# A fused two-layer decoder: three-pass products ordered with the pass outermost, and one transpose moved to another PSUM bank

## Chip, core and metric

The kernel runs on one core of one Trainium2 chip, as a single program. The metric is device time in microseconds of that core; the time before is the median of three runs. Every time below is from one profiled execution unless it is called a run's time.

## The reference

The reference is a decoder of two layers over 512 tokens of 1,024 features, all in fp32. The first layer's mixer is a latent attention (low-rank queries and keys with a rotary part), the second's a sliding-window attention with 16 query heads and 4 key heads. Each mixer and each MLP is followed by a layer normalisation of a scaled residual:

```python
def _mlp(x, w_up, w_down):
    h = jax.nn.relu(x @ w_up)
    return (h * h) @ w_down

for l in range(DEPTH):                      # DEPTH = 2
    y = _mla(x, ...) if l < n_a else _swa(x, ...)
    x = _layernorm(alpha * x + y, ln_mix_g[l], ln_mix_b[l])
    x = _layernorm(alpha * x + _mlp(x, mlp_w_up[l], mlp_w_down[l]), ...)
```

The hidden width is 4,096, so the two MLPs hold most of the arithmetic. The latent attention also has `c_q = _rmsnorm(h[..., :384], g_q)`, the query latents, of which the kernel needs the transpose.

## The kernel before, in words

**Three passes.** TensorE multiplies in a reduced fp32 format, so each fp32 operand is split into a high and a low part (`split`, line 74: ScalarE copies the high part on line 76, VectorE subtracts it from the source on line 79 and so makes the low part). A product is then three matmuls, which `three` (line 107) lists and `group` (line 101) issues in that order: stationary high with moving high, stationary high with moving low, stationary low with moving high. Nearly every matmul of the kernel is issued by line 103 in `group`. The names in the trace are the tiles' names: `wh` and `wl` are the high and low part of a weight tile, `xth` and `xtl` those of the transposed activations, `fac` holds both parts of a factor of the hidden activations.

**The MLP.** One level of a seven-product block scheme is used for each of four blocks of the hidden width (`Block`, line 682), for the up products of all four and the down products of the first three; the fourth block's down product is a plain one (`TokMajor`). A step of kind U with number n (`up`, line 701) makes one of the seven up products of a block: 128x128 pieces of the weight are stationary and 256 columns of activations move; it takes two weight tiles, each of eight pieces, so it issues 48 matmuls into two PSUM banks, one for each weight tile. A step of kind D (`down_`, line 760) makes one of the seven down products: pieces of the factor are stationary and 512 columns of a weight tile move; it takes two weight tiles and two row tiles t of 128 tokens, and issues 24 matmuls into two banks, one for each row tile. Before, `up` ran over four output pieces j (two to a weight tile), in each over four contraction pieces k, and for each k the three passes. `down_` ran over the row tile t, in it over four contraction pieces m (the first two from the first weight tile, the other two from the second), and for each m the three passes; behind the twelve matmuls of one t it read that bank out with VectorE (lines 548 and 551 for the residual, 778 and 781 for a partial sum kept in `u2`).

**The order of the steps** is written out by hand in `STEPS`, `FIRST_STEPS` and `LAST_STEPS` (lines 39 and 40). Each MLP begins with U1 U2 U5 U3 U6 U7 D2 U4 D1 of block 0, then U1 of block 1, D5 of block 0, U2, D3, U5 and so on. In the text a step is named by its kind and number, and by the layer (A the first, B the second).

**Weight tiles** come through a ring of four pairs `wh` and `wl` (`tiles_of_weights`, line 116). A raw tile is loaded by a DMA from the SP queue, or grown in place by an accumulating DMA from the POOL queue (line 184); then it is split. `weights` (line 293) prepares tiles up to four ahead on the ring. All matmuls stand in the order of the program; the other engines' instructions are put in order when the program is built, by a planner that uses its own estimates of time.

**PSUM.** There are six product banks (tag mm, `bank`, line 65) and two for transposes (tag tr, `tbank`, line 68). U6 uses the two transpose banks, all other steps product banks. VectorE combines the banks of U5, U3 and U6 on lines 736 to 742 (line 737 reads U5's banks, line 739 U3's).

**Where layer B begins.** `begin` (line 567) makes the shared keys and the first queries with `feat_major` (line 561): three chunks of weights, for each of two halves of the tokens, eight contraction pieces of 256 columns in two groups of four. Transposes of the last token tiles, which make the end of `x2`'s `xth` and `xtl`, are put between these groups.

**The third latents.** `normed_t` (line 875) transposes the query latents, three features pieces f of 128; f = 0 and 1 in one call, f = 2 in the next. Each piece takes a transpose bank, is scaled by ScalarE (line 880) and has its low part made by VectorE (line 881).

Of the kernel before, what the change touches and what calls it, by code (L numbers as in the profile page):

```python
# [2 lines left out]

# [12 lines left out]
P = 128  # L16
D = 1024
S = 512
NT = S // P
KD = D // P  # L20
# [28 lines left out]
def build(tc, nc, io, out):  # L49
    with ExitStack() as top:  # L50
# [17 lines left out]
        def tbank():  # L68
            return bank(512, "tr", 2)
# [31 lines left out]
        def group(dst, pairs, first=True, last=True, **kw):  # L101
            for i, (st, mv) in enumerate(pairs):
                pe(nc.tensor.matmul(  # L103
                    dst, st, mv, start=first and i == 0, stop=last and i == len(pairs) - 1, **kw
                ))

        def three(sh, sl, mh, ml):
            return [(sh, mh), (sh, ml), (sl, mh)]


        stream, off_ring = [], []
# [218 lines left out]
        b = bank()  # L330
# [227 lines left out]
            add_plain(t, c, b)  # L558
            count(t, c)

        def feat_major(src, w, dst, cols=slice(0, S), ks=range(KD)):
            wh, wl = w
            for k in ks:
                kc = slice(k * P, (k + 1) * P)
                group(dst, three(wh[:, kc], wl[:, kc], src.h(k, cols), src.l(k, cols)), k == 0, k == KD - 1)

        def begin(src, chunks):


            ws = [weights(name) for name, _ in chunks]  # L570
            for half_ in range(2):
                cols = slice(half_ * 256, half_ * 256 + 256)
                for i, (_, evac) in enumerate(chunks):
                    b = bank(256)
                    early = half_ == 0 and i == len(chunks) - 1
                    feat_major(src, ws[i], b, cols, range(4))
                    if early:
                        with tc.high_priority():
                            last = src.turn(NT - 1, bank)
                    feat_major(src, ws[i], b, cols, range(4, KD))  # L580
                    evac(cols, b)
                    if half_ == 0 and i == 1:
                        with tc.high_priority():
                            src.turn(NT - 2)
                if half_ == 0:
                    with behind(last):
                        prepare(1)
            state["hold"] = len(stream)


        class Factors:
# [9 lines left out]
            def sum(self, n, a11, a12, a21, a22):  # L601
                if n == 5:
                    self.a = self.scratch()
                    nc.vector.tensor_sub(self.a, a21, a22)
                    return self.a
                if n == 3:
                    nc.vector.tensor_sub(self.a, self.a, a11)
                    self.b = self.scratch()
                    nc.vector.tensor_add(self.b, a12, self.a)
                    return self.b  # L610
                if n == 7:
                    nc.vector.tensor_sub(self.b, a11, a21)
                    return self.b
                return {1: a11, 2: a12, 4: a22, 6: self.a if n == 6 else None}[n]
# [49 lines left out]
        def mlp(src, gb, dst, mp):  # L664
# [17 lines left out]
            class Block:  # L682
# [18 lines left out]
                def up(self, n):  # L701
                    w = [weights("up") for _ in range(2)]
                    key = {3: 3}.get(n) or own_bank[n]
                    for j in range(4):

                        b = self.bank(("U", key), j // 2)
                        wh, wl = w[j // 2]
                        for k in range(4):
                            c = slice(j % 2 * 512 + k * P, j % 2 * 512 + (k + 1) * P)
                            group(  # L710
                                b[:, j % 2 * 256 : j % 2 * 256 + 256],
                                three(wh[:, c], wl[:, c], src.part(n, 0)[:, k, :], src.part(n, 1)[:, k, :]),
                                n not in (2, 4) and k == 0 and j % 2 == 0, k == 3, skip_group_check=True,
                            )
                        if j % 2:
                            self.up_out(n, j // 2)
                        if (self.q, j) == (0, 1) and n in (1, 2):
                            with tc.high_priority():
                                src.turn(n + 1)

# [39 lines left out]
                def down_(self, n):  # L760
                    w = [weights("down") for _ in range(2)]
                    f = self.fac.pop(n)
                    key = {3: 5}.get(n) or own_bank[n]
                    if self.q == 0 and n == 2:
                        key = 2
                    for t in range(2):
                        tk = slice(t * P, (t + 1) * P)
                        b = self.bank(("D", key), t)
                        for m in range(4):
                            wh, wl = w[m // 2]  # L770
                            c = slice(m % 2 * 512, (m % 2 + 1) * 512)
                            group(
                                b, three(f[:, 0, m, tk], f[:, 1, m, tk], wh[:, c], wl[:, c]),
                                (n not in (2, 3, 4) or key == 2) and m == 0, m == 3, skip_group_check=True,
                            )
                        add = add_scaled if self.q == 0 else add_plain
                        if n == 1 and self.q == 0:
                            nc.vector.tensor_copy(u2[t], b)
                            add_plain(t, lows, b)
                        elif n in (1, 6):  # L780
                            nc.vector.tensor_add(u2[t], b, u2[t])
                        elif n == 2:
                            add(t, lows, b)
                        elif n == 5:
                            add(2 + t, highs, b)
                        elif n == 3:
                            add(t, highs, b)
                        elif n == 7:
                            take(2 + t, highs, b)
                        elif n == 4:  # L790
                            add(2 + t, lows, b)
# [53 lines left out]
        with tc.tile_pool(name="mla", bufs=1) as mp:  # L845
# [28 lines left out]

            def normed_t(nrm, fs, g, dst_h, dst_l):
                for f in fs:
                    pt = tbank()
                    for t in range(NT):
                        pe(nc.tensor.transpose(pt[:, t * P : (t + 1) * P], nrm[t][:, f * P : (f + 1) * P], ident))
                    nc.scalar.activation(dst_h[:, f, :], pt, AF.Copy, scale=g[:, f : f + 1])  # L880
                    nc.vector.scalar_tensor_tensor(
                        dst_l[:, f, :], pt, g[:, f : f + 1], f32(dst_h[:, f, :]), ALU.mult, ALU.subtract
                    )
# [160 lines left out]
            for t in range(NT):  # L1044
                tk = slice(t * P, (t + 1) * P)
                b = bank()
# [403 lines left out]
```

## Time and profile before

| what | before |
|---|---|
| median of three runs | 1002.6 us (1002.33 to 1003.85) |
| the profiled execution's own time | 1002.69 us |
| its span, first to last instruction | 1000.9 us |
| TensorE matmul busy | 988.5 us, 99% of the span |
| VectorE, ScalarE, GpSimd busy | 77%, 55%, 24% |
| mean granted TensorE clock | 0.997 of full speed |

Two instructions of one engine overlap in the profile where the second begins before the first has ended, as matmuls do; the distance between the starts of neighbouring matmuls is therefore what tells the pace, and a longer distance than usual is a stall. In a timeline row the first number is the start in microseconds from the span's start, the second the time covered, x the number of instructions merged, and a bracket holds the idle time of the engine just before and what ended it.

### The profile page before, as it was taken

How to read it: one execution, taken by the hardware profiler on the slowest of the kernel's cores; microseconds unless marked ns; L12 is line 12 of the kernel's file. 1: busy time of each engine (PE TensorE's matmuls, PEld its weight loads, DVE VectorE, ACT ScalarE, POOL GpSimd, SP SyncE). 2: the span in 40 equal slices, each digit the busy share in tenths (PEclk: the TensorE clock that was granted, in tenths of full speed). 3: DMA queues.
4: the chain of work that ended last, by engine and by line, in shares of the span. 5: the costliest groups of instructions: out<-in, count | busy, mean ns of one | idle time of the engine just before them, and what ended most of it. 6: DMA issues, size and time to landing. Idle time of an engine off the chain costs nothing. (4 is left out here: it accounts for less than half of the span.)

```text
span 1000.9 us, 15857 instructions
## 1 busy us (share of the span) xinstructions
PE 988.5 (99%) x6148; PEld 891.6 (89%) x6148; DVE 767.3 (77%) x1231; ACT 555.0 (55%) x847; POOL 236.0 (24%) x208
## 2 busy tenths in 40 slices
PE   9999999999999999999999999999999999999996
PEld 9888888998999999998899988889988999999986
DVE  6588866989769769886584678788995986898746
ACT  5556643467537637646146688546673664664610
POOL 1231101312212211210024565233122122123002
PEclk9999999999999999999999999999999999999998
DMA  7421125388978977973323211439698798798332
GB/s 260 143 87 43 64 106 190 84 191 236 186 168 229 185 175 203 221 125 112 120 67 113 85 64 54 153 79 228 172 217 196 167 215 175 162 262 147 83 126 84
DMA packets 60246, 149.55 MB, mean 149 GB/s; under 512 B 5211, under 2 KB 9740, under 8 KB 60172
## 3 DMA queue, kind: packets, MB, share of 16 engines
q0 software_dynamic: 24320, 58.73, 32.7%
q1 hardware_dynamic: 35852, 89.82, 26.1%
q8 instruction: 48, 0.79, 0.3%
q14 instruction: 26, 0.21, 0.1%
HBM read 146.41 MB, written 4.22 MB: 150 GB/s over the span
## 5 line engine op out<-in xcount | busy, mean ns | idle before, releaser
L103 PE MATMUL mm<-wh,fac 128*128 128x512 f32 (+1 forms) x944 | 293.1, 387 | 0.0
L76 ACT ACTIVATE wh<-wq 128x1024 fp32r<-128x1024 f32 x164 | 173.7, 1061 | 189.6 <-PE mm L103 126.3
L79 DVE TENSOR_TENSOR wl<-wq,wh 128x1024 fp32r<-128x1024 f32 x164 | 199.5, 1221 | 76.7 <-ACT wh L76 75.8
L103 PE MATMUL mm<-xth,wh 128*128 128x256 f32 (+1 forms) x936 | 244.9, 289 | 0.0
L103 PE MATMUL mm<-xth,wl 128*128 128x256 f32 (+1 forms) x808 | 234.6, 290 | 0.0
L103 PEld LDWEIGHTS mm<-wh,fac 128*128 128x128 f32 x944 | 176.2, 188 | 35.7 <-DVE fac L79 0.6
L103 PE MATMUL mm<-xtl,wh 128*128 128x256 f32 (+1 forms) x680 | 198.8, 292 | 0.3 <-DVE xtl L79 0.3
L103 PE MATMUL mm<-wl,fac 128*128 128x512 f32 (+1 forms) x472 | 182.6, 387 | 1.0 <-DVE wl L79 1.0
L103 PEld LDWEIGHTS mm<-xth,wh 128*128 128x128 f32 x936 | 170.3, 192 | 3.0
L103 PEld LDWEIGHTS mm<-xth,wl 128*128 128x128 f32 x808 | 154.8, 192 | 2.3
L184 POOL DMA_DIRECT2D wq<-in_up x64 | 77.5, 1219 | 244.6 <-DVE wl L79 179.2
L103 PEld LDWEIGHTS mm<-xtl,wh 128*128 128x128 f32 x680 | 130.2, 192 | 3.5 <-DVE xtl L79 0.7
L76 ACT ACTIVATE wh<-raw 128x1024 fp32r<-128x1024 f32 (+2 forms) x81 | 81.8, 1015 | 78.6 <-PE mm L103 57.6
L103 PEld LDWEIGHTS mm<-wl,fac 128*128 128x128 f32 x472 | 88.8, 188 | 18.3 <-DVE wl L79 1.7
L79 DVE TENSOR_TENSOR wl<-raw,wh 128x1024 fp32r<-128x1024 f32 (+2 forms) x60 | 72.4, 1218 | 33.3 <-ACT wh L76 32.7
L184 POOL DMA_DIRECT2D wq<-in_down x48 | 42.0, 875 | 204.9 <-DVE wl L79 182.2
L391 POOL TENSOR_TENSOR rs<-v,half 128x1 f32<-128x1 f32 x24 | 28.7, 1197 | 191.1 <-DVE v L410 156.1
L79 POOL TENSOR_TENSOR wl<-raw,wh 128x1024 fp32r<-128x1024 f32 (+2 forms) x21 | 43.8, 2092 | 72.6 <-ACT wh L76 72.6
L103 PE MATMUL mm<-wh,oh 128*128 128x512 f32 x128 | 51.0, 398 | 0.7 <-ACT p L1252 0.7
L103 PE MATMUL mm<-wh,ol 128*128 128x512 f32 x128 | 50.1, 391 | 0.0
L103 PE MATMUL mm<-wl,oh 128*128 128x512 f32 x128 | 49.9, 390 | 0.0
L551 DVE TENSOR_TENSOR x<-mm,x 128x512 f32<-128x512 f32 (+1 forms) x53 | 35.7, 676 | 13.8 <-PE mm L103 13.5
(227 smaller groups left out, 1834.8 us busy)
## 6 DMA issues: line engine op xcount, KB each, us to landing
wq<-in_up POOLq DMA_DIRECT2D x64, 512.0 KB, 8.5
wq<-in_down POOLq DMA_DIRECT2D x48, 512.0 KB, 7.3
wq<-in_up SPq DMA_DIRECT2D x32, 512.0 KB, 5.6
raw<-in_down SPq DMA_DIRECT2D x28, 512.0 KB, 6.5
wq<-in_down SPq DMA_DIRECT2D x24, 512.0 KB, 7.4
raw<-in_up SPq DMA_DIRECT2D x16, 512.0 KB, 5.8
raw<-in_w_o SPq DMA_DIRECT2D x8, 512.0 KB, 3.3
raw<-in_w_so SPq DMA_DIRECT2D x8, 512.0 KB, 3.5
```

The lines of the kernel that those rows point to most:

```text
L76: high = nc.scalar.activation(dst_h, src, AF.Copy)
L79: low = (engine or nc.vector).tensor_sub(dst_l, src, f32(dst_h))
L103: pe(nc.tensor.matmul(dst, st, mv, start=first and i == 0, stop=last and i == len(pairs) - 1, **kw))
L184: nc.gpsimd.dma_start(half(a, jp), chunk(*more, jp), accum_op=ALU.add)
L391: nc.gpsimd.tensor_tensor(r, v, half, ALU.pow)
L551: nc.vector.tensor_add(xs[t][:, c], b, xs[t][:, c])
```

## The change

In `up`, `down_` and the products of `begin` the pass becomes an outer loop. In `up` the order is now weight tile, pass, output piece j, contraction piece k. In `down_` it is weight tile i, pass p, row tile t, contraction piece m within the weight tile; so both row tiles' banks are open through the whole step, and both are read out behind its last matmul. In `begin` each group of four contraction pieces is issued pass by pass. The number, shapes and operands of all matmuls stay. In `normed_t` the piece f = 2 takes a product bank and no longer a transpose bank.

```diff
+        def by_pass(chunks):
+
+            return [chunk[n] for n in range(3) for chunk in chunks]
...
-        def feat_major(src, w, dst, cols=slice(0, S), ks=range(KD)):
+        def feat_major(src, w, dst, cols=slice(0, S), ks=range(KD), order=lambda chunks: sum(chunks, [])):
             wh, wl = w
+            chunks = []
             for k in ks:
                 kc = slice(k * P, (k + 1) * P)
-                group(dst, three(wh[:, kc], wl[:, kc], src.h(k, cols), src.l(k, cols)), k == 0, k == KD - 1)
+                chunks.append(three(wh[:, kc], wl[:, kc], src.h(k, cols), src.l(k, cols)))
+            group(dst, order(chunks), ks[0] == 0, ks[-1] == KD - 1)
...
-                    feat_major(src, ws[i], b, cols, range(4))
+                    feat_major(src, ws[i], b, cols, range(4), by_pass)
...
-                    feat_major(src, ws[i], b, cols, range(4, KD))
+                    feat_major(src, ws[i], b, cols, range(4, KD), by_pass)
...
                     key = {3: 3}.get(n) or own_bank[n]
-                    for j in range(4):
-
-                        b = self.bank(("U", key), j // 2)
-                        wh, wl = w[j // 2]
-                        for k in range(4):
-                            c = slice(j % 2 * 512 + k * P, j % 2 * 512 + (k + 1) * P)
-                            group(
-                                b[:, j % 2 * 256 : j % 2 * 256 + 256],
-                                three(wh[:, c], wl[:, c], src.part(n, 0)[:, k, :], src.part(n, 1)[:, k, :]),
-                                n not in (2, 4) and k == 0 and j % 2 == 0, k == 3, skip_group_check=True,
-                            )
-                        if j % 2:
-                            self.up_out(n, j // 2)
-                        if (self.q, j) == (0, 1) and n in (1, 2):
+                    for i in range(2):
+                        b = self.bank(("U", key), i)
+                        wh, wl = w[i]
+                        for p in range(3):
+                            for j, k in product(range(2), range(4)):
+                                c = slice(j * 512 + k * P, j * 512 + (k + 1) * P)
+                                group(
+                                    b[:, j * 256 : j * 256 + 256],
+                                    three(wh[:, c], wl[:, c], src.part(n, 0)[:, k, :], src.part(n, 1)[:, k, :])[p : p + 1],
+                                    n not in (2, 4) and (p, j, k) == (0, 0, 0), (p, k) == (2, 3), skip_group_check=True,
+                                )
+                        self.up_out(n, i)
+                        if (self.q, i) == (0, 0) and n in (1, 2):
                             with tc.high_priority():
                                 src.turn(n + 1)
...
+                    for i, p, t, m in product(range(2), range(3), range(2), range(2)):
+                        tk, c, k = slice(t * P, (t + 1) * P), slice(m * 512, (m + 1) * 512), 2 * i + m
+                        wh, wl = w[i]
+                        group(
+                            self.bank(("D", key), t), three(f[:, 0, k, tk], f[:, 1, k, tk], wh[:, c], wl[:, c])[p : p + 1],
+                            (n not in (2, 3, 4) or key == 2) and (i, p, m) == (0, 0, 0), (i, p, m) == (1, 2, 1),
+                            skip_group_check=True,
+                        )
                     for t in range(2):
-                        tk = slice(t * P, (t + 1) * P)
                         b = self.bank(("D", key), t)
-                        for m in range(4):
-                            wh, wl = w[m // 2]
-                            c = slice(m % 2 * 512, (m % 2 + 1) * 512)
-                            group(
-                                b, three(f[:, 0, m, tk], f[:, 1, m, tk], wh[:, c], wl[:, c]),
-                                (n not in (2, 3, 4) or key == 2) and m == 0, m == 3, skip_group_check=True,
-                            )
...
-                    pt = tbank()
+                    pt = bank() if f == 2 else tbank()
```

## Rows read from the trace of the kernel before

**Rows 1.** The page's part 1: busy time, share of the span and instructions of each engine.
```profile
PE 988.5 (99%) x6148; PEld 891.6 (89%) x6148; DVE 767.3 (77%) x1231; ACT 555.0 (55%) x847; POOL 236.0 (24%) x208
```
**Rows 2.** Waits of TensorE: us in total, times, longest us.
```profile
PE mm L103 <- DVE wl L79: 1.0, 2, 0.8
```
**Rows 3.** Timeline of TensorE, from layer A's first D5 into the U2 behind it.
```profile
248.26 0.50 PE L103 MATMUL mm<-wl,fac 128*128 128x512 f32 x1 [0.76 <-DVE wl L79]
...
252.26 0.28 PE L103 MATMUL mm<-xth,wh 128*128 128x256 f32 x1
252.38 0.28 PE L103 MATMUL mm<-xtl,wh 128*128 128x256 f32 x1
252.50 0.28 PE L103 MATMUL mm<-xth,wl 128*128 128x256 f32 x1
```
**Rows 4.** Stretches of a step each: length, then busy time (instructions) by engine.
```profile
245.56:252.26 6.70, 5.94 (x26) 4.43 (x25) 5.68 (x7) 6.33 (x7) 1.32 (x2) 1.00 1.11 255
729.67:735.68 6.01, 5.77 (x27) 4.44 (x25) 5.67 (x7) 5.96 (x7) 1.73 (x2) 1.00 1.10 258
258.02:263.49 5.47, 5.47 (x27) 4.51 (x26) 3.49 (x5) 3.68 (x4) 2.92 (x3) 1.00 1.02 187
252.26:258.02 5.76, 5.76 (x50) 5.75 (x48) 5.76 (x6) 3.56 (x4) 1.24 (x2) 1.00 1.00 183
199.89:205.84 5.95, 5.95 (x51) 5.82 (x49) 5.12 (x8) 5.74 (x8) 1.20 (x1) 1.00 1.06 302
683.94:689.95 6.01, 6.01 (x50) 5.82 (x49) 5.25 (x8) 5.86 (x8) 1.20 (x1) 1.00 1.06 306
```
**Rows 5.** Timeline of VectorE, the split before each late matmul of D5, layers A and B.
```profile
246.98 1.23 DVE L79 TENSOR_TENSOR wl<-wq,wh 128x1024 fp32r<-128x1024 f32 x1 [1.02 <-ACT wh L76]
...
730.41 1.22 DVE L79 TENSOR_TENSOR wl<-wq,wh 128x1024 fp32r<-128x1024 f32 x1 [0.34 <-ACT wh L76]
```
**Rows 6.** Timeline of VectorE and TensorE at U5 of layer B and in `begin`.
```profile
683.46 1.29 DVE L79 TENSOR_TENSOR xtl<-uv,xth 128x512 fp32r<-128x512 f32 x2
...
521.52 0.28 PE L103 MATMUL mm<-xth,wh 128*128 128x256 f32 x1
522.15 0.39 PE L103 MATMUL mm<-xtl,wh 128*128 128x256 f32 x1 [0.34 <-DVE xtl L79]
522.37 0.28 PE L103 MATMUL mm<-xth,wl 128*128 128x256 f32 x1
```
**Rows 7.** Timeline of TensorE at the third latents' transposes.
```profile
45.69 0.40 PE L103 MATMUL mm<-wh,ckv_l 128*128 128x512 f32 x1
46.26 0.66 PE L879 MATMUL tr<-ident,p 128*128 128x128 f32 x4 [0.17 <-DVE cq_l L881]
```
**Rows 8.** Timeline of VectorE and TensorE where D2 of layer B begins.
```profile
707.04 0.68 DVE L737 TENSOR_TENSOR uv<-mm,uv 128x512 f32<-128x512 f32 x1
707.23 0.40 PE L103 MATMUL mm<-wh,fac 128*128 128x512 f32 x1
```
**Rows 9.** Timeline of VectorE and TensorE around the last D4 of layer B.
```profile
947.75 0.69 DVE L551 TENSOR_TENSOR x<-mm,x 128x512 f32<-128x512 f32 x1
949.26 0.69 DVE L551 TENSOR_TENSOR x<-mm,x 128x512 f32<-128x512 f32 x1 [0.82 <-PE mm L103]
949.87 1.22 DVE L79 TENSOR_TENSOR wl<-raw,wh 128x1024 fp32r<-128x1024 f32 x1
951.00 1.22 DVE L79 TENSOR_TENSOR fac<-a,fac 128x1024 fp32r<-128x1024 f32 x1
...
952.27 0.73 PE L103 MATMUL mm<-wh,fac 128*128 128x512 f32 x2
```
**Rows 10.** Waits of all engines, then a split and its step in the middle of layer A.
```profile
ACT wh L76 <- PE mm L103: 186.1, 133, 5.8
...
341.95 1.23 DVE L79 TENSOR_TENSOR wl<-wq,wh 128x1024 fp32r<-128x1024 f32 x1 [1.76 <-ACT wh L76]
...
347.77 0.40 PE L103 MATMUL mm<-wh,fac 128*128 128x512 f32 x1
```

More of the change, by code (lines that the diff above doesn't have):

```diff
@@ L1 @@
 import math
+from itertools import product
 from contextlib import ExitStack
```

## The prediction

> **What bounds the kernel now.** The first view is the share of busy time by engine: TensorE's matmuls cover 99% of the span, no other engine more than 77% [rows 1]. That view can't show how fast the matmuls follow each other, so the second is TensorE's timeline, read by starts. In U2 of layer A neighbouring matmuls of 256 columns start 0.12 us apart [rows 3], and the step of 48 takes 5.76 us, 0.120 each; D3, 24 matmuls of 512 columns, takes 5.47 us, 0.228 each [rows 4]. Almost all steps run at these two paces, so TensorE is the bound and the change, which adds and removes no matmul, can win only what stands between matmuls. The third view, TensorE's waits, shows how little that is: it waits 1.0 us in all for low parts of weights, two times [rows 2], and the other waits are below a microsecond. So the question is which of these stalls the new order hides and whether it opens others.
>
> **The change, part by part.** The sum is made against the profiled execution, 1002.69 us (span 1000.9); the median of the runs is 1002.6, so 0.1 comes off at the end.
>
> *1. Down products, D5 of block 0.* It takes 6.70 us in layer A and 6.01 in layer B, against 5.47 for a free step: 1.23 and 0.54 us are lost [rows 4]. The late matmul starts at 248.26 behind 0.76 us of idleness, released by VectorE's low part [rows 3]; that split ran from 246.98 for 1.23 us, to 248.21 [rows 5]. It is the step's eighth matmul: row tile 0 has used the first weight tile in its first six and now wants the second tile's low part. In the new order the first tile feeds twelve matmuls, and the second tile's low part is wanted at the seventeenth: 245.56 + 16 x 0.228 = 249.21, which is 1.0 us behind its readiness. In layer B it is ready at 730.41 + 1.22 = 731.63 [rows 5] and wanted at 729.67 + 3.65 = 733.32. Both stalls go: 1.77 us. Bounds: nothing, if the splits slip by more than those leads, up to 1.77; I take 1.77, because the leads of 1.0 and 1.7 us are larger than anything that I find added in front of the splits below. What is late next? Behind D5 the splits run far ahead again: a split in the middle of layer A ends at 341.95 + 1.23 = 343.18 for a step that starts at 347.77, a lead of 4.6 us, and ScalarE's high parts wait 186.1 us in all for TensorE to give ring tiles back [rows 10]. TensorE holds the splits up there, not they it.
>
> *2. Up products, U5 of block 0.* It takes 5.95 and 6.01 us against 5.76: 0.19 and 0.25 lost [rows 4]. Here the low part of the activations is late: in layer B VectorE makes two from 683.46 for 1.29 us [rows 6], to 684.75, the first about 684.15, and the step starts at 683.94 with the low part wanted by its second matmul. In the new order eight matmuls come first, 8 x 0.12 = 0.96 us, so it is wanted at 684.90, behind even the second. Gain 0.44; bounds 0 and 0.44. In all other U steps the weights' low part is wanted 14 matmuls later than before and the high part is given back seven matmuls earlier (its last use, the 23rd matmul of a tile's 24, becomes the 16th); nothing waits there now, so this is costed at nothing.
>
> *3. The first products of layer B.* From 521.52 to the second matmul at 522.15 are 0.63 us where 0.12 is the pace, and the next distance is 0.22: 0.61 lost, released by a low part of activations [rows 6]. Pass by pass that low part is wanted by the fifth matmul, 521.52 + 0.48 = 522.00, still 0.15 early. So 0.15 stays, and perhaps the 0.10 behind it: gain 0.36 to 0.46, I take 0.40.
>
> *4. The third latents.* The four transposes start 0.57 us behind the matmul before them, where 0.23 is the pace; the release is VectorE's low part of the latents before, which frees the transpose bank [rows 7]. A product bank needs no such wait if one of the six is free. Gain 0 to 0.34; I take 0.34, since among TensorE's stalls around this place none was released by the reading of a product bank.
>
> Parts 1 to 4: 1.77 + 0.44 + 0.40 + 0.34 = 2.95 us.
>
> *5. Two banks at once in a down step.* Row tile 1's bank is wanted by the third matmul, not the thirteenth: 10 x 0.228 = 2.3 us earlier. In the regular order a bank has been read out a whole step before. The tight place is D2 of block 0, which follows U6 and U7, whose banks VectorE is still reading: in layer B the second read of U5's banks runs from 707.04 for 0.68 us, to 707.72, and D2 starts at 707.23, so its third matmul comes at 707.69 [rows 8]. Which bank the planner gives can't be seen before; and TensorE will be there up to 0.25 earlier (part 2). So 0 to about 0.5 us a layer; I take 0.15 for each, 0.30, because the read ends almost exactly when it is wanted.
>
> *6. Read-outs behind the step.* Row tile 0's read-out, 0.69 us of VectorE, moves from the middle of the step to its end, next to row tile 1's. In the middle of an MLP this lies beside splits that lead by 4.6 us [rows 10], so it costs nothing; without that cover it would cost up to 0.69 a step. At the last D4 there is no cover. The read-outs run at 947.75 and 949.26, then a weight's and a factor's low part, the latter until 951.00 + 1.22 = 952.22, and TensorE takes it up at 952.27 [rows 9]. The first read-out can now start two matmuls ahead of the second, about 949.26 - 0.46 = 948.80. Two in a row at a distance of 0.60 then end the pair about 0.15 later, and the factor with it. Two layers: 0.30; bounds 0 and 2 x 0.69 = 1.38.
>
> By this sum the change gives 2.95 - 0.30 - 0.30 = 2.35 us: 1002.69 - 2.35 = 1000.34, and 1000.3 beside the median. Every queue keeps its instructions: no DMA is added, and SP's and POOL's loads hang on splits that come no later than now, apart from what part 6 says.
>
> **A rule against it.** The rows show that the read-out of one row tile now runs beside the other row tile's matmuls, and that the splits lead by more than that read-out takes. The Trainium skill, "Perfetto Trace Analysis", section "Matmuls", asks that independent groups rotate through PSUM banks, so that the read-out of one overlaps the matmuls of the next; the change gives half of that up. By that rule each of the 42 down steps (seven in three blocks of two layers) would lay one read-out of 0.69 us open, 29 us in all, and the sum would be 1002.69 + 29 - 2.95, about 1029. The rows speak against the full price: the group behind a D step uses other banks, and the overlap is with that. What is left of the rule is the second rival.
>
> **The rivals.**
>
> *Given back, no difference.* The stalls move. For: the leads at the start of each MLP are 1 us, VectorE's read-outs are bunched, and with all of parts 5 and 6 at their upper ends (1.0 + 1.38) the gain is 2.95 - 2.38 = 0.57, so 1002.1. The same follows where D5's stall stays in part: the two read-outs behind D2 and D1 (D1's row tile 0 has two, so 0.69 + 1.37 = 2.06) pushing D5's second split past its lead of 1.0 in layer A would leave most of the 1.23. Against: that split waits for ScalarE [rows 5], so VectorE has a free place in front of it. This rival includes that the change does less than it says, since only D5's stalls are waits for a low part of weights. Between 1000.6 and 1004.6, most likely near 1001.7. Chance 0.35.
>
> *Slower, by read-outs in front of splits.* Place: VectorE's queue in the first nine steps of each MLP. If its fixed order puts both read-outs of D2, D1 and D5 ahead of splits that are wanted at once, each step pays in full: 0.69 + 1.37 + 0.69 = 2.75 a layer, 5.5 in all, against 2.95 gained: 1002.69 + 2.55 = 1005.2. It decides where a split's lead is below the read-out's 0.69 us. For: D5's lead is nearly nothing today. Against: the new order itself adds over 2 us to that lead (parts 1 and 2), and elsewhere it is 4.6. Chance 0.12.
>
> **How the numbers follow.** The forecast case, 999.4 to 1000.6, has the remaining 0.53; its lower end is 1002.6 - 3.2, all stalls of parts 1 to 4 gone with the 0.25 left in part 3. About 0.2% (2.0 us) is what a measurement of this kernel can tell from no change, so faster means below 1000.6: 0.53, within 0.35, slower 0.12. The range runs from 999.2 to 1003.0: it takes in the forecast and nearly all of the first rival and leaves out the second. The forecast's own range is 999.4 to 1000.6.
>
> **What would show it.** In the profile after: D5 of block 0 at 5.47 us in both layers, with no wait of TensorE for a weight's low part (part 1); U5 of block 0 at 5.76 (part 2); one wait of some 0.15 us at the first products of layer B (part 3); no wait at the third latents (part 4). A wait of TensorE for VectorE's line 737 or 739 at the third matmul of D2 would price part 5, and a later factor split behind the last D4 part 6. The forecast is wrong if the paces of 0.120 and 0.228 us change with the order of the passes, or if new waits of TensorE for splits, factors or banks add up to more than 0.9 us, where the gain falls below 2.0.

## The result, and the profile after

The changed kernel takes 1011.2 us (median of four runs, 1009.82 to 1012.48) against 1002.6: a ratio of 1.0083, 95% interval 1.0067 to 1.0099. It is slower, and well outside the range of the prediction. The profiled execution is the longest of the four, 1012.48 us, its span 1010.7, at the same mean clock (0.997).

TensorE still covers nearly all of the span and the number of its instructions is the same. Page, part 1, of the kernel after, against [rows 1]:

```profile
PE 990.4 (98%) x6148; PEld 891.1 (88%) x6148; DVE 766.6 (76%) x1231; ACT 552.2 (55%) x847; POOL 236.0 (23%) x208
```

The paces have not changed: a free U step still takes 48 x 0.120 us, a D step 24 x 0.228. So the loss lies between the matmuls. Take each distance between the starts of two neighbouring matmuls, less the usual (median) distance for the size of the first (0.120 us for 256 columns, 0.227 for 512), and add the differences up: 12.0 us before, 21.8 after. That is 9.8 us more, and the profiled executions differ by 1012.48 - 1002.69 = 9.8. Of it 4.9 and 5.0 us are in the U and D steps of layers A and B; the rest cancels. What is lost at a place, here and below, is counted in this way. TensorE's waits, of the kernel after, name the new stalls (us in total, times, longest us), against [rows 2]:

```profile
PE mm L104 <- DVE u L787: 5.1, 4, 1.3
PE mm L104 <- DVE uv L743: 2.4, 2, 1.4
...
PE mm L104 <- ACT fac L77: 1.0, 3, 0.5
...
PE mm L104 <- ACT wh L77: 0.5, 1, 0.5
```

No wait for a weight's low part is left, as predicted. But there are three others in the MLPs. (Line numbers moved: VectorE's split is now line 80, ScalarE's 77, the reads of the banks of U6, U5 and U3 are lines 742, 743 and 745, the partial sum's read-out 787.)

**First, D2 waits for D1.** In blocks 1 and 2 D2 adds onto the banks that D1 has just filled, after VectorE has added the partial sum to `u2` (line 787). Timelines of TensorE and then VectorE, kernel after, from the end of U4 of block 1 into D2 (a row's x4 are the four matmuls of one pass over one weight tile):

```profile
307.75 1.12 PE L104 MATMUL mm<-xth,wl 128*128 128x256 f32 x8
309.12 1.20 PE L104 MATMUL mm<-wh,fac 128*128 128x512 f32 x4 [0.25 <-ACT fac L77]
...
313.78 1.07 PE L104 MATMUL mm<-wh,fac 128*128 128x512 f32 x4
316.15 1.25 PE L104 MATMUL mm<-wh,fac 128*128 128x512 f32 x4 [1.30 <-DVE u L787]
```
```profile
307.20 1.22 DVE L80 TENSOR_TENSOR wl<-raw,wh 128x1024 fp32r<-128x1024 f32 x1 [0.48 <-ACT wh L77]
308.90 0.69 DVE L751 TENSOR_TENSOR a<-mm,uv 128x512 f32<-128x512 f32 x1 [0.48 <-PE mm L104]
309.51 2.35 DVE L80 TENSOR_TENSOR fac<-a,fac 128x1024 fp32r<-128x1024 f32 x2
...
314.18 1.22 DVE L80 TENSOR_TENSOR wl<-wq,wh 128x1024 fp32r<-128x1024 f32 x1
315.32 1.28 DVE L787 TENSOR_TENSOR u<-mm,u 128x512 f32<-128x512 f32 x2
```

D1's last matmul starts at about 314.46 and D2's first would follow 0.23 us later. It comes at 316.15, because it must follow the read-out, and a weight's split (314.18) stands in front of the read-out (315.32) in VectorE's queue: 1.46 us lost here, 1.40, 1.45 and 1.42 at the other three places, 5.7 in all. Before, the read-out of row tile 0 lay beside D1's matmuls of row tile 1, and that of row tile 1 beside D2's matmuls of row tile 0. VectorE's timeline, kernel before, same place:

```profile
312.82 0.69 DVE L781 TENSOR_TENSOR u<-mm,u 128x512 f32<-128x512 f32 x1
...
314.66 0.68 DVE L781 TENSOR_TENSOR u<-mm,u 128x512 f32<-128x512 f32 x1
```

**Second, U7 of the last block waits for U5's banks.** Timelines of ScalarE, VectorE and TensorE, kernel after, at U6 and U7 of layer A's last block:

```profile
451.01 1.06 ACT L77 ACTIVATE wh<-wq 128x1024 fp32r<-128x1024 f32 x1 [1.63 <-DMA wq<-in_up]
```
```profile
450.55 0.68 DVE L742 TENSOR_TENSOR uv<-tr,uv 128x512 f32<-128x512 f32 x1
452.10 1.23 DVE L80 TENSOR_TENSOR wl<-wq,wh 128x1024 fp32r<-128x1024 f32 x1 [0.87 <-ACT wh L77]
453.24 0.68 DVE L743 TENSOR_TENSOR uv<-mm,uv 128x512 f32<-128x512 f32 x1
```
```profile
454.07 1.19 PE L104 MATMUL mm<-xth,wh 128*128 128x256 f32 x8 [0.95 <-DVE uv L743]
```

Between the reads of U6's and U5's banks stands a split that waits for ScalarE, which waits for a load. Before, the two reads stood side by side. VectorE's timeline, kernel before, same place:

```profile
446.01 0.69 DVE L736 TENSOR_TENSOR uv<-tr,uv 128x512 f32<-128x512 f32 x1 [0.68 <-PE tr L103]
446.74 0.69 DVE L737 TENSOR_TENSOR uv<-mm,uv 128x512 f32<-128x512 f32 x1
```

Lost: 1.10 us in layer A, 1.59 in B.

**Third, D1 waits for its factor** (at 309.12 above, and at the other three D1 of blocks 1 and 2), 0.4 to 0.5 us each with the matmul behind, 1.8 in all. ScalarE's timeline, kernel after: the raw weight tile of D2 (306.13), wanted only at 316, and a square (307.08, line 754) that D5 will use go ahead of the high part of D1's factor (the first half of the row at 308.02; the second is D2's factor), wanted at 308.7.

```profile
306.13 1.04 ACT L77 ACTIVATE wh<-raw 128x1024 fp32r<-128x1024 f32 x1
307.08 1.04 ACT L754 ACTIVATE a<-a 128x1024 f32<-128x1024 f32 x1
308.02 1.99 ACT L77 ACTIVATE fac<-a 128x1024 fp32r<-128x1024 f32 x2
```

D5 of block 0 answers to [rows 4]: in layer A its stall became a wait for its factor (0.66 us, and 0.11 behind it); in B it is gone. (The first stretch begins one matmul, 0.12 us, before the step would.)

```profile
245.96:252.34 6.38, 5.88 (x28) 4.62 (x27) 6.35 (x7) 6.32 (x8) 0.86 (x1) 1.00 1.10 267
...
200.42:206.18 5.76, 5.76 (x50) 5.76 (x49) 4.94 (x8) 5.55 (x8) 1.13 (x1) 1.00 1.06 304
688.85:694.61 5.76, 5.76 (x51) 5.76 (x50) 4.99 (x8) 5.61 (x8) 1.20 (x1) 1.00 1.06 302
```

The second and third row are U5 of block 0 in both layers, now free steps of 5.76 us.

### The profile page after: what moved, and what is told of

It reads as the page before. It is cut to its first block, busy times and chain, and to the rows that moved or that the text cites. A ratio compares the mean times of both kernels' runs of the same rounds, so it can differ in the third digit from the quotient of the medians.

```text
span 1010.7 us, 15861 instructions
## 1 busy us (share of the span) xinstructions
PE 990.4 (98%) x6148; PEld 891.1 (88%) x6148; DVE 766.6 (76%) x1231; ACT 552.2 (55%) x847; POOL 236.0 (23%) x208
## 4 chain that ended last, share of the span: by engine, by line
PE 49%; issue 32%; POOL 8%; DMA 4%; DVE 4%; ACT 2%; POOLq 0%; SPq 0%; DVEq 0%; ACTq 0%
PE mm L104 45%; POOL wq L189 7%; DMA wq<-in_up 2%; DVE wl L80 1%; DMA wq<-in_down 1%; ACT wh L77 1%; PE tr L1102 1%; PE tr L1278 1%; PE tr L648 1%; PE tr L104 1%; DMA xw<-in_xT 1%; PE tr L1280 0%; ACT p L1258 0%; DMA raw<-in_w_qr 0%; DMA raw<-in_w_h 0%
## 5 line engine op out<-in xcount | busy, mean ns | idle before, releaser
L104 PE MATMUL mm<-wh,fac 128*128 128x512 f32 (+1 forms) x944 | 254.2, 388 | 6.3 <-DVE u L787 5.1
L104 PEld LDWEIGHTS mm<-wh,fac 128*128 128x128 f32 x944 | 173.3, 188 | 43.1 <-ACT fac L77 8.9
L104 PE MATMUL mm<-xth,wh 128*128 128x256 f32 (+1 forms) x936 | 143.9, 290 | 2.4 <-DVE uv L743 2.4
L104 PE MATMUL mm<-wl,fac 128*128 128x512 f32 (+1 forms) x472 | 141.3, 386 | 0.0
L104 PEld LDWEIGHTS mm<-xth,wh 128*128 128x128 f32 x936 | 124.9, 191 | 6.7 <-issue 2.7
L104 PE MATMUL mm<-xth,wl 128*128 128x256 f32 (+1 forms) x808 | 128.4, 290 | 0.0
L104 PE MATMUL mm<-xtl,wh 128*128 128x256 f32 (+1 forms) x680 | 110.6, 292 | 0.0
L104 PEld LDWEIGHTS mm<-xth,wl 128*128 128x128 f32 x808 | 107.9, 192 | 2.3
L104 PEld LDWEIGHTS mm<-xtl,wh 128*128 128x128 f32 x680 | 91.4, 192 | 1.9 <-DVE xtl L80 0.2
```

The source lines that it names most:

```text
L104: pe(nc.tensor.matmul(dst, st, mv, start=first and i == 0, stop=last and i == len(pairs) - 1, **kw))
```

## The experiments

The theory after the result had two parts. *Bank*: D2 of blocks 1 and 2 can't start until D1's banks are read, and the new order of the down products puts both read-outs behind D1's last matmul. *Queue*: the new order of the up products gives the high part of a weight tile back seven matmuls earlier; ring tiles come free sooner, and the planner then puts splits that are not yet wanted ahead of reads and factors that are. Rivals were that passes outermost are slow in themselves, or that VectorE and ScalarE simply have no room.

In the first four, what is put back is as in the kernel before. Line numbers differ by a few between the kernels.

### The up products alone

```diff
-                    for i, p, t, m in product(range(2), range(3), range(2), range(2)):
+                    for t in range(2):
...
-                    feat_major(src, ws[i], b, cols, range(4), by_pass)
+                    feat_major(src, ws[i], b, cols, range(4))
...
-                    pt = bank() if f == 2 else tbank()
+                    pt = tbank()
```

> Only the up products go pass by pass; down products, the first products of layer B and the third latents as before. Theory (queue): giving high parts of weights back earlier moves splits ahead of read-outs in the fixed queues of VectorE and ScalarE, and this belongs to the up order alone: the waits at U7 of the last block (1.1 and 1.6 us) and at D1 of blocks 1 and 2 (some 1.8 us in all) stand here too, the waits of D2 for D1's read-outs do not, and D5 of block 0 still stalls; 1002.6 + 2.7 + 1.8 - 0.4 = 1006.7 us. Rival (read-outs): all of the loss comes from reading both banks out behind a down step: then nothing is lost here and U5's 0.4 us is won, 1002.2 us.

Measured: 1010.2 us, ratio 1.0071 (1.0058 to 1.0085). Timeline of TensorE in this kernel, D1 of block 1:

```profile
308.53 0.50 PE L104 MATMUL mm<-wh,fac 128*128 128x512 f32 x1
...
310.33 0.73 PE L104 MATMUL mm<-wh,fac 128*128 128x512 f32 x2 [1.06 <-DVE fac L80]
```

The four D1 of blocks 1 and 2 lose 6.4 us to waits for their factor (7.2 with the 0.11 behind each), more than in the changed kernel, because the old order of the down products wants the factor's low part at the third matmul and not the ninth. U7 loses only 0.20 and 0.25. So the queue's price was larger than expected (1006.7), and it sat mostly at D1 and not at U7. D5 of block 0, expected to stall as before, loses only 0.18 us in layer A (1.14 in the kernel before) and 0.56 in B.

### The down products alone

The loop of `up`, the calls in `begin` and the bank of the third latents are put back; `down_` stays new:

```diff
-                        for p in range(3):
-                            for j, k in product(range(2), range(4)):
...
+                    for j in range(4):
...
+                        for k in range(4):
```

> Only the down products go weight tile by weight tile; all else as before. Theory (bank): D2 of blocks 1 and 2 adds onto D1's banks and must wait until VectorE has read D1's partial sum, four waits of 1.4 us, 5.7 in all, and D5's 1.8 us are won: 1002.6 + 5.7 - 1.8 = 1006.5 us, with no wait at U7 or for D1's factor. Rival (read-outs): the whole loss is here, near 1011 us, with the waits at U7 and D1 as well.

Measured: 1009.8 us, 1.0070 (1.0055 to 1.0086). TensorE's waits in this kernel:

```profile
PE mm L104 <- DVE u L788: 1.7, 4, 0.4
PE mm L104 <- ACT fac L77: 1.5, 2, 0.8
```

D2's four waits are there (0.58 us lost at each, 0.15 more at the matmuls behind). But they make less than 3 us: here the split in front of the read-out starts 1.2 us before D1's last matmul (314.11 and 315.31) and is over in time, in the changed kernel 0.3 before it. The other part is at D5 of block 0, where the wait for a weight's low part has become one for the factor: 0.86 and 0.97 us at its first matmul, 0.36 and 0.35 at its ninth. Stalls in the two MLPs rise by 4.5 us, outside them by 1.3; the profiled execution is the shortest of the four runs (1008.53 us), so 1.2 us of the median's loss are not in this trace. The total lies between the two expectations: the bank is confirmed as a place, not as the whole loss.

The two losses do not add up: 7.6 and 7.1 us apart, 8.6 together. Together D1 loses 1.8 us and not 6.4, while D2's waits grow from 2.9 to 5.7 and those of U7 from 0.45 to 2.7.

### The first products of layer B and the third latents alone

The loops of `up` and `down_` are put back, the rest of the change stays:

```diff
-                    for i in range(2):
...
-                        for p in range(3):
+                    for j in range(4):
...
-                    for i, p, t, m in product(range(2), range(3), range(2), range(2)):
...
                     for t in range(2):
...
+                        for m in range(4):
```

> Only the first products of layer B go pass by pass and the third latents take a product bank; up and down products as before. Both theories: the gains of 0.4 and 0.3 us stand by themselves, 1001.9 us, with a wait of about 0.15 us left in the first products. If either is taken back, 1002.6 us.

Measured: 1002.1 us, 0.9993 (0.9984 to 1.0002). In the trace the wait at the third latents is gone, and at the first products 0.25 of 0.61 us is left, as expected. By the ratio this gains 0.7 us, less than a measurement can tell from none.

### The same, and the new order only in U5 and D5 of block 0

```diff
+                    if (n, self.q) == (5, 0):
+                        self.up_passes(n)
+                    else:
+                        self.up_pieces(n)
...
+                    if (n, self.q) != (5, 0):
+                        self.down_rows(n)
+                    else:
+                        self.down_tiles(n)
```

> As e3_begin_f2, and the new order in U5 and D5 of block 0 alone, the two steps of each layer that stalled before. Theories queue and bank: neither price is paid, because no D2 follows a D1 in the new order and nearly all high parts are given back where they were, so the whole of the forecast gain comes, 1002.6 - 2.9 = 999.7 us. If D5's stall is not a matter of order but of when its second tile arrives, it stays at some 1 us in layer A and the time is 1000.7 to 1001.5 us.

Measured: 1000.6 us, 0.9975 (0.9966 to 0.9985): faster than both kernels, but 0.9 us above what was expected and next to the range named for a D5 that stays late (1000.7 to 1001.5). The trace decides: no stall of over 0.15 us is left in D5 and U5 of block 0. Timelines of VectorE and TensorE in this kernel, D5 of layer A:

```profile
247.46 1.23 DVE L80 TENSOR_TENSOR wl<-wq,wh 128x1024 fp32r<-128x1024 f32 x1 [0.94 <-ACT wh L77]
```
```profile
246.12 1.09 PE L104 MATMUL mm<-wh,fac 128*128 128x512 f32 x4
...
249.78 1.07 PE L104 MATMUL mm<-wl,fac 128*128 128x512 f32 x4
```

The split of the second tile ends at 248.69 and is wanted at 249.78: a lead of 1.1 us.

### The order of two instructions in the queues

The up products alone (the first experiment), with two instructions placed behind the split of D1's factor at the U4 of blocks 1 and 2. `behind` only orders the instructions of a queue.

```diff
-                    w = [weights("up") for _ in range(2)]
+                    late = self.pair if n == 4 and 0 < self.q < NFF - 1 else None
+                    w = [weights("up")]
+                    with behind(late):
+                        w.append(weights("up"))
...
-                        self.up_out(n, i)
+                        with behind(late if i else None):
+                            self.up_out(n, i)
...
-                    split(f[:, 0], f[:, 1], g[2] if n == 0 else self.down.sum(n, *g))
+                    self.pair = split(f[:, 0], f[:, 1], g[2] if n == 0 else self.down.sum(n, *g))
```

> The new order in the up products everywhere (as in the run with it alone, 1010.2 us), and at the four U4 of blocks 1 and 2 two instructions go behind the split of D1's factor in their queues: the split of the raw weight tile that D2 will use, and VectorE's second read-out of U4. Nothing else is moved; no matmul, load or buffer changes. Theory (the early give-back only spoils the order of the queues): TensorE's waits for the factor at D1, 6.5 us in that run, go, and the time falls to about 1003.7 (1003.0 to 1005.0). Rival (the factor is late because ScalarE and VectorE are loaded more at that place, or the pass order itself costs time): the waits stay or move behind D1, to D2's weights, and the time stays at 1009 to 1010.5.

Measured: 1006.3 us, 1.0030 (1.0018 to 1.0042), against 1.0071 without the edit; the intervals do not meet. The losses at D1 fall from 6.4 to 1.45 us. What is left is order in the queues again, with another instruction. Timelines of ScalarE and TensorE in this kernel:

```profile
306.47 1.99 ACT L758 ACTIVATE a<-a 128x1024 f32<-128x1024 f32 x2
308.36 1.04 ACT L77 ACTIVATE fac<-a 128x1024 fp32r<-128x1024 f32 x1
309.31 1.04 ACT L77 ACTIVATE wh<-raw 128x1024 fp32r<-128x1024 f32 x1
```
```profile
310.72 0.73 PE L104 MATMUL mm<-wh,fac 128*128 128x512 f32 x2 [0.53 <-DVE fac L80]
```

The raw tile (309.31) is now behind the high part of D1's factor (308.36). But two squares stand ahead of it (306.47), of which D1 needs one; the kernel before makes the other, which D5 will use, behind that factor (at 309.45, the factor at 306.60). So the factor's low part comes 0.7 us too late for D1's third matmul (310.72), and less than that at the other three D1. The time is 1.3 us above the upper end of what was expected; 0.55 and 0.28 us are lost at U7, 0.35 at D2 of block 0 in layer B, and the first 20 us took 1.1 us longer than in the first experiment's profile.

### Passes outermost, but the high part used to the end

The up products alone again, with the passes taken in another order:

```diff
-                        for p in range(3):
+                        for p in (0, 2, 1):
...
-                                    n not in (2, 4) and (p, j, k) == (0, 0, 0), (p, k) == (2, 3), skip_group_check=True,
+                                    n not in (2, 4) and (p, j, k) == (0, 0, 0), (p, k) == (1, 3), skip_group_check=True,
```

> The new order in the up products everywhere, but the three passes of a weight tile taken as high by high, low by high, high by low, so that the weight's high part is used to the tile's end, as before, and its low part is wanted at the ninth matmul. Theory (giving the high part back seven matmuls earlier is what lets splits move ahead): the queues' order stays that of before, D1 has its factor as before, and the time is that of before less the 0.44 us of U5: about 1002.3 (1001.8 to 1003.0). Rival (passes outermost are slower in themselves, or the release has nothing to do with it): 1008 to 1010.

Measured: 1002.8 us, 1.0003 (0.9994 to 1.0012). The whole loss of 7 us is gone with the early release, although the passes are still outermost. VectorE's timeline of this kernel at D1 of block 1: the factor's low part (307.45) is again ahead of the second read-out of U4 and of the raw tiles.

```profile
307.45 2.36 DVE L80 TENSOR_TENSOR fac<-a,fac 128x1024 fp32r<-128x1024 f32 x2 [0.50 <-ACT fac L77]
309.73 0.69 DVE L751 TENSOR_TENSOR a<-mm,uv 128x512 f32<-128x512 f32 x1
310.33 2.35 DVE L80 TENSOR_TENSOR wl<-raw,wh 128x1024 fp32r<-128x1024 f32 x2
```

This edit also moves the use of the low part from a tile's seventeenth matmul to its ninth. No wait for a weight's low part loses over 0.5 us in either kernel, so that does not explain 7 us.

### D2 in banks of its own

The changed kernel, with:

```diff
-                    if self.q == 0 and n == 2:
+                    if n == 2:
                         key = 2
...
                             nc.vector.tensor_add(u2[t], b, u2[t])
+                            if n == 1:
+                                add_plain(t, lows, b)
```

> The changed kernel, but D2 adds onto no bank of D1 any more: in all blocks it has banks of its own, as in block 0, and VectorE adds D1's banks into the output a second time (eight read-outs more in all, 0.69 us each). Theory (D2 waits until VectorE has read the partial sum out of D1's bank, 1.4 us at each of four places): these 5.7 us go, and 1011.2 falls to about 1005.5 (1005 to 1007). Rival (VectorE is simply behind at that place, so that any bank or factor wanted there comes late): the waits move to the next step's banks or to D5's factor, and the time stays above 1009.

Measured: 1005.8 us, 1.0027 (1.0016 to 1.0039), against 1.0083: the 5.7 us are gone at D2 of blocks 1 and 2, as expected, though VectorE does eight read-outs more. TensorE's waits in this kernel show where one came back:

```profile
PE mm L104 <- DVE uv L743: 3.4, 3, 1.3
```

Two are the U7 from above (1.09 and 1.49 us lost); the third is D2 of block 0 in layer B, 1.29 us lost at its first matmul for U5's bank.

### All three repairs

The last experiment's kernel with the edit of the queues from above, and the low part of one weight tile of the last block's U4 (the split in front of line 743) made by GpSimd (`low` is handed on to `split`; those lines are left out here):

```diff
-            4: lambda jp: grown("a", jp),
+            4: lambda jp: grown("a", jp, low=nc.gpsimd if jp in late else None),
...
-            add = {("U", q): queue_seven("up", "U", up(q)) for q in range(NFF)}
+            add = {("U", q): queue_seven("up", "U", up(q), (0,) if q == NFF - 1 else ()) for q in range(NFF)}
```

> The changed kernel with three repairs: D2 in banks of its own; at U4 of blocks 1 and 2 the raw tile's split and the second read-out behind the split of D1's factor; and the low part of one weight tile of the last block's U4 made by GpSimd and not by VectorE, so that U5's banks are read without a split between. Theory: 1011.2 less 5.7 (D2), 1.8 (D1) and 2.7 (U7) is 1001.0 (1000.3 to 1002.0), level with the run that has the new order in D5 and U5 of block 0 alone. Rival (VectorE has no room for the new order, whichever instruction stands where): the waits come back at other places and the time stays above 1004.

Measured: 1002.0 us, 0.9993 (0.9984 to 1.0002), just above the upper end of what was expected and 9.2 us below the changed kernel. TensorE's longest waits in it:

```profile
PE mm L104 <- POOL zeros L334: 1.4, 1, 1.4
PE mm L104 <- ACT p L1264: 0.7, 1, 0.7
PE mm L104 <- DVE ql L80: 0.6, 2, 0.3
```

All three are outside the MLPs, and in the kernel before too. So VectorE and ScalarE have room for the new order; the order of their queues and one pair of banks cost the time. But this is no better than the kernel before, and 1.4 us behind the one whose MLPs use the new order at two steps of a layer.

## Why the prediction was wrong

**The step that failed first** is in part 5: "In the regular order a bank has been read out a whole step before." It holds for every pair of down steps that share banks but D1 and D2 of blocks 1 and 2, which stand next to each other. The code says so: n = 2 takes D1's key except in block 0, and 787 reads the bank in between. The prediction priced two banks at once only at D2 of block 0 (0.30 us); no wait came there in the changed kernel, while 5.7 us came at four places that it had not listed. Had D1's banks been followed, rows of before gave a price: in the new order D1's last matmul for row tile 0 is the 22nd of 24 and starts 3 x 0.227 = 0.68 us before D2; it takes 0.40 [rows 8] and the read-out 0.69 [rows 9], so D2 comes at least 0.4 us late at each of four places. The down products alone show 0.58 and 0.15 behind it, 2.9 in all, which is more than the forecast gain of 2.35; with a split in front of the read-out it is 5.7.

**The second** is in part 2: the earlier release of the high part, "nothing waits there now, so this is costed at nothing", and with it, behind part 6, "SP's and POOL's loads hang on splits that come no later than now". TensorE did not wait, but ScalarE did: 186.1 us in all for ring tiles [rows 10]. So the ring held ScalarE's splits back, and with the release they went ahead of something. In these fixed queues they went ahead of D1's factor (6.4 us with the up products alone, 1.8 in the changed kernel, where the down products want the factor's low part later) and of the read of U5's banks (2.7). That factor had little room: the prediction took 4.6 us as the lead in the middle of an MLP, from one weight split, but the factor's low part led by 0.2 us at D1 of block 1 in layer A, and by 0.9 at the other three. VectorE's timeline, kernel before (D1's factor is the first of the two, ready at 308.90; D1's third matmul starts at 309.11):

```profile
307.68 2.36 DVE L79 TENSOR_TENSOR fac<-a,fac 128x1024 fp32r<-128x1024 f32 x2 [1.02 <-ACT fac L76]
```

For the up products alone the experiment with the late release shows that the release is the cause, and the one with two instructions moved that the order of the queues is how it acts at D1. At U7 the traces of all kernels side by side show the same, and what sets the size:

| kernel | split between the reads of U6's and U5's banks | ScalarE's copy for it, us behind U6's start (layers A, B) | lost at U7 (A, B) |
|---|---|---|---|
| before; down products alone; first products and third latents alone; new order in U5 and D5 only; high part used to the end | no | | none |
| up products alone | yes | 2.9, 2.9 | 0.20, 0.25 |
| two instructions moved | yes | 3.2, 3.0 | 0.55, 0.28 |
| D2 in banks of its own | yes | 3.8, 4.2 | 1.09, 1.49 |
| changed kernel | yes | 3.8, 4.3 | 1.10, 1.59 |

The early release puts the split there, and the later its tile is copied, the more it costs. No run took that split away by itself; the wait is gone in the kernel with all three repairs, of which only GpSimd's low part touches that block. Why the copy comes later with both new orders is open.

**Part 1** was right for the weight's low part where the new order is used at U5 and D5 alone: a lead of 1.1 us, where 1.0 was worked out. In the changed kernel that wait is gone too, but in layer A by luck: the splits slipped, and the low part is ready at 250.34, 0.16 us before it is wanted at 250.50. Had the step begun on time it would have been wanted at about 249.7. Timelines of VectorE and TensorE, kernel after:

```profile
249.12 1.22 DVE L80 TENSOR_TENSOR wl<-wq,wh 128x1024 fp32r<-128x1024 f32 x1
```
```profile
250.50 1.09 PE L104 MATMUL mm<-wl,fac 128*128 128x512 f32 x4
```

What held the step up was the factor. It was late in layer A of the changed kernel, and in both layers with the down products alone; part 1 left it out. Timelines of VectorE and ScalarE, kernel after, ahead of D5 of layer A:

```profile
243.18 0.68 DVE L784 COPY u<-mm 128x512 f32<-128x512 f32 x1
243.78 0.68 DVE L556 TENSOR_TENSOR x<-mm,x 128x512 f32<-128x512 f32 x1
244.38 1.21 DVE L611 TENSOR_TENSOR uv<-a,a 128x1024 f32<-128x1024 f32 x1
```
```profile
245.63 1.06 ACT L77 ACTIVATE fac<-uv 128x1024 fp32r<-128x1024 f32 x1 [2.67 <-DVE uv L611]
```

Two read-outs of D1's banks stand ahead of the sum that the factor is made of, and ScalarE waits for the sum. With the new order at U5 and D5 alone both stalls go; that run is 1.4 us faster than the one without these two steps (1002.07 less 1000.63), where 1.77 + 0.44 was the sum. Between the two profiles the losses in the MLPs fall by 2.0 us, near that sum, and those outside rise by 0.3.

**Parts 2 (U5), 3 and 4** came as worked out: U5 at 5.76 us in both layers, 0.14 + 0.10 us left at the first products of layer B where 0.15 to 0.25 was forecast, no wait at the third latents. Timelines of TensorE, kernel after, against [rows 6, 7]:

```profile
526.80 0.65 PE L104 MATMUL mm<-xth,wh 128*128 128x256 f32 x4
527.43 0.74 PE L104 MATMUL mm<-xtl,wh 128*128 128x256 f32 x4
```
```profile
46.27 0.39 PE L104 MATMUL mm<-wh,ckv_l 128*128 128x512 f32 x1
46.50 0.60 PE L885 MATMUL mm<-ident,p 128*128 128x128 f32 x4
```

**Part 6** (0.15 us a layer at the last D4) cost nothing in the changed kernel; 0.19 and 0.18 appeared with the down products alone.

**One reading** of the waits was not right: "the other waits are below a microsecond" leaves out 1.4 us for the tile of zeros at the very start. The change does not touch it.

**The rule against it** was the better guide than its price. The Trainium skill, "Perfetto Trace Analysis", section "Matmuls", asks that independent groups rotate through PSUM banks so that the read-out of one overlaps the matmuls of the next. The prediction answered that the group behind a D step uses other banks. Where that is so no step lost anything to it; at the one pair where the second group adds onto the first one's bank, so that the two are not independent, the read-out lay open, at 0.6 us (down products alone) to 1.5 a time: there the traces bear out what the rule is for.

**The rivals.** "Slower, by read-outs in front of splits" had the sign but not the mechanism: the damage came from splits in front of read-outs and factors, in blocks 1 to 3 and not in the first nine steps. Read-outs in front cost something only at D5 of block 0 (0.77 us in layer A), a step behind the place that the rival named. It was given 0.12. "Given back, no difference" priced the read-outs at 1.0 + 1.38 us at most, and its case of D5 held up by them came in layer A, by way of the factor; the 5.7 us at D2 lay outside it.

## What to carry to other kernels

For each buffer that a change lets go sooner or holds longer, list the next writer of that same buffer, every instance of it; "usually read a step earlier" hides the instance where it isn't. An engine that waits long for buffers is being held back by them: to give them back sooner can change what stands in front of what in the fixed queues, so the leads to list are those of all that is wanted there, factors and read-outs too, and not of weight splits alone. In this kernel the new order paid where the stall was (two steps of a layer, with the first products and the third latents 0.9975) and not everywhere (1.0083).

## What the runs showed of the hardware

A wait of TensorE costs more than its idle time. At D1 in the changed kernel the idle time is 0.25 us (309.12 above), but it is counted from the end of the matmul before; from start to start 0.41 us are lost, and 0.11 more behind the first matmul: the four matmuls that start at 309.12 cover 1.20 us, and four of the same kind without a wait 1.09 (246.12 above).

Second, the first 20 us, which hold none of the edited steps, lose between 2.3 us (kernel before) and 3.9 (the run with two instructions moved). Some 2 us of that are no wait. The first ten matmuls, on a tile of zeros, start 0.43 us apart, where 512 columns start 0.227 apart later. TensorE's timeline, kernel before:

```profile
1.42 4.64 PE L103 MATMUL mm<-zeros 128*128 128x512 f32 x10 [1.42 <-POOL zeros L329]
```

That is the pace of the lower of the clock's two levels (1.2 and 2.4 GHz). The trace's record of the granted clock begins, at full speed, 6.0 us behind the span's start here, where the pace doubles; a profile's clock of 1.00 for the stretch before that is no reading. In the ten profiles the record begins between 4.9 and 7.6 us. A wait for the first weights comes on top: it loses under 0.1 us in the kernel before and 1.2 in the run with two instructions moved. Both differ from profile to profile, so one profile alone can't settle a difference below about 1.6 us.
